# The tables of an S5 layer: spread rows read back by DMA, or products with states on partitions and a transpose on TensorE

## The chip, the cores and the metric

One Trainium2 chip, one of its cores. The metric is the device time of one launch in microseconds (us). The engines are called TensorE (PE in the profile, its weight loads PEld), VectorE (DVE), ScalarE (ACT), GpSimd (POOL) and SyncE (SP); each works through its own list of instructions in order and waits on semaphores for the others. SyncE only issues DMAs here; GpSimd computes and issues DMAs as well.

## The reference

One inference step of a decoder of two layers, for 256 prompt tokens and 8 samples of one token (264 columns in all), model width 2048, in float32. Layer 0 mixes with retention and HGRN2 heads, layer 1 with S5; after each mixer comes a SwiGLU FFN of width 5632.

The S5 layer has 128 groups of 16 channels with 64 complex states each:

```
dt = exp(log_dt);  a = exp(lam * dt);  b' = ((a - 1) / lam) * b      (complex, for each group and state)
h[t] = a * h[t-1] + b' u[t]                                          (u: 16 channels of the group)
y[t] = Re(c h[t]) + d * u[t]
```

followed by a GELU and a gated linear layer (GLU). The kernel doesn't scan token by token. It takes chunks of 8 tokens and makes two tables for each group out of a, b', c: `wb` takes the 8 x 16 inputs of a chunk to its 64 complex states and to the chunk's own outputs, `wc` takes the states to the outputs of the next 8 tokens.

## The kernel before

**The stream.** All large products run as one stream of units through `Step.stream` (lines 102 to 135). A unit is up to 8 blocks of 128x128 weights, 512 KB. SyncE loads it into one of 4 buffers `raw` (`load`, L82); ScalarE rounds it to the matmul format, `whi` (L88), and the rest `wlo = raw - whi` is made by VectorE, or by GpSimd for every `S.every`-th unit (`split`, L95). TensorE then does three matmuls a block on 264 columns (L126, L127, L129). `ahead` keeps splits up to 4 units and loads up to 8 units in front of the unit in work. Results are taken from PSUM by VectorE (gate L1544, up L1551 to L1554, w_dn L1559).

**Tasks beside the stream.** After each unit `Step.slot` calls every active generator once (`next`). A generator writes a few instructions into the engines' lists and yields. So the number of yields sets beside which unit a piece of work stands; a unit is all that lies between two calls.

**The first FFN** has 272 units: 64 of gate and up, 32 of w_dn, 64, 32, 48, and 32 short ones (6 blocks). Beside it runs `s5_tables` (L810), then the first part of `s5` (L1182), which loads finished tables back for the S5 stage. `s5_tables` makes, in this order:

- a, b' and their factors for all groups, states on partitions, 64 columns (two groups' states fill the 128 partitions); `S.every = 3` from here on;
- the rotations `rot`, 32 powers of a unit number (L938 to L965), wide products on VectorE;
- the powers of a, `pw`, and their products with the states' factor, `pdc`; these are transposed (L988) and written to DRAM (`pdd`); the coefficients b with the norm's gain, made on GpSimd (L1002), go to DRAM too (`btd`);
- `S.every = 0`, and the samples' part (a h0, L1014 to L1066);
- a loop over 16 groups of tables (`kt`), 8 S5 groups each, 9 calls a pass (5 in the first).

In a pass, GpSimd makes `bb` (b' with the gain) from the loaded coefficients `bc`; VectorE makes `T`, the table from states to tokens (L1151 to L1164), which goes to DRAM as `wc` (L1170). `through` (L1091) multiplies `bz` and `T` on TensorE (L1097) to the block within the chunk, `kp`, written to DRAM in 8 pieces (L1106). `spread` (L1084) lets SyncE load two tiles of 128x1024, `us` (a row of `pdd` for each token, the same on 16 partitions) and `vs` (a row of `btd` for each channel, repeated for 8 tokens); `tokens` (L1109) multiplies them on VectorE, complex, to the part of wb from tokens to states, which is written to DRAM as it stands (L1118), a piece of it to `bn` (L1122).

**After the stream,** `s5` makes the tokens' norm factors; while it waits, 10 matmuls on a tile of constants are put on TensorE (L1277). The S5 stage loads `wb` and `wc` through SyncE into whatever buffers are free.

Of the kernel before, what the change touches and what calls it, by code (L numbers as in the profile page):

```python
# [10 lines left out]
F32 = mybir.dt.float32  # L11
# [35 lines left out]
class Step:  # L47
    """The chip's state while the program is written out: pools, the stream of weights, the tasks beside it."""
# [183 lines left out]
def layer0(S, I, O):  # L232
# [206 lines left out]
    # the heads' products of earlier with later tokens, [(earlier), chunk, later]; never written above the diagonal  # L439
# [6 lines left out]
    def hg_head(h, H):  # L446
# [9 lines left out]
        def decay(l):  # L456
            """Takes the pairs of blocks to blocks of 2^l: the left keys to the block's end, the right queries to its start."""
# [154 lines left out]
    # the first four blocks together: they wait for the norm anyway  # L612
# [3 lines left out]
    # head start  # L616
# [192 lines left out]

def s5_tables(S, I):  # L810
    """The S5 layer's tables, beside the first FFN: chunks of 8 tokens, for each of the 128 groups
    from tokens to states and within the chunk (wb), and from states to tokens (wc)."""
# [52 lines left out]
    # sine and cosine - 1 of a quarter of the angle, doubled twice  # L865
# [59 lines left out]
    # the multiplier of a chunk and the unit rotations of its phase  # L925
# [4 lines left out]
    yield  # L930
# [3 lines left out]
    rot = S.rot  # L934
    G.memset(rot[:, 0, :, 0:1], 1.0)
    G.memset(rot[:, 1, :, 0:1], 0.0)
    cc, k = col("cc"), col("a0")
    n = 1  # L938
    while n < 32:
        # back to length 1, or its errors would grow with the chunks  # L940
        ts(cc, cm, 1.0, None, op0=OP.add)
        V.tensor_mul(p, cc, cc)
        V.tensor_mul(k, s, s)
        V.tensor_add(p, p, k)
        ts(p, p, -0.5, 1.5, op0=OP.mult, op1=OP.add)
        V.tensor_mul(s, s, p)
        V.tensor_mul(cc, cc, p)
        ts(cm, cc, -1.0, None, op0=OP.add)
        yield
        if n == 1:  # L950
            V.tensor_copy(rot[:, 0, :, 1:2], one(cc))
            V.tensor_copy(rot[:, 1, :, 1:2], one(s))
        else:
            w = min(n, 8)
            slow = n > 4
            for off in range(0, n, w):
                t = [new(f"rt{i}", [128, 64, 8])[:, :, :w] for i in range(2)]
                bc = lambda v: one(v).to_broadcast([128, 64, w])
                for _ in cmul(V, [rot[:, i, :, n + off:n + off + w] for i in range(2)],
                              [rot[:, i, :, off:off + w] for i in range(2)], (bc(cc), bc(s)), t):  # L960
                    if slow:
                        yield
        n *= 2
        if n < 32:
            double(s, cm)  # L965
            yield
    # powers of a
# [5 lines left out]
    # what wb takes from the states and what it takes from the channels, turned and spread by DMA:  # L973
    # the powers, falling with the token, times the states' factor
    pd, pdc = (new(n, [128, 2, KT, 8, 4]) for n in ("pd", "pdc"))
    for j in range(8):
        A.activation(pd[:, :, :, j], pw[:, :, :, 7 - j].rearrange("p i (k q) -> p i k q", q=4), AF.Copy)
        if j % 4 == 3:
            yield
    t = [new(f"rt{i}", [128, 64, 8]).rearrange("p a b -> p (a b)").rearrange("p (k j q) -> p k j q", j=8, q=4)  # L980
         for i in range(2)]
    cb = [v.rearrange("p (k o q) -> p k o q", o=1, q=4).to_broadcast([128, KT, 8, 4]) for v in (cr, ci)]
    yield from cmul(V, [pdc[:, i] for i in range(2)], [pd[:, i] for i in range(2)], cb, t)
    pdt = pd.rearrange("p i k j q -> p (i k j q)").rearrange("p (b r i s) -> p b r i s", b=4, r=2, i=2)
    for b in range(4):
        p = S.pt()
        for i in range(2):
            PE.transpose(p[:, 128 * i:128 * i + 128], pdc[:, i, 4 * b:4 * b + 4].rearrange("p k j q -> p (k j q)"), S.ident)  # L988
        A.activation(pdt[:, b], p[:, :256].rearrange("p (i r s) -> p r i s", i=2, r=2), AF.Copy)
        yield  # L990
    pdd = S.dr.tile([KT, 8, 1024], F32, name="pdd", bufs=1)
    G.dma_start(bass.AP(tensor=pdd.tensor, offset=pdd.offset, ap=[[256, 128], [32768, 4], [1, 256]]),
                pdt.rearrange("p b r i s -> p b (r i s)"))
    gt = new("gt", [128, KT])
    G.dma_start(gt, I["s5g"])
    btd = S.dr.tile([KT, 16, 1024], F32, name="btd", bufs=1)
    for b in range(4):
        bt = new(f"rt{b % 2}", [128, 64, 8]).rearrange("p a b -> p (a b)").rearrange("p (k x) -> p k x", k=4)
        G.dma_start(bt, I["s5b"][:, 4 * b:4 * b + 4])
        yield  # L1000
        yield
        G.tensor_mul(bt, bt, gt[:, 4 * b:4 * b + 4].rearrange("p (k o) -> p k o", o=1).to_broadcast([128, 4, 128]))  # L1002
        G.dma_start(bass.AP(tensor=btd.tensor, offset=btd.offset + 65536 * b, ap=[[128, 128], [16384, 4], [1, 128]]), bt)
# [24 lines left out]
    for h in range(2):  # L1028
# [34 lines left out]
    ym = new("rt0", [128, 64, 8])[:, :32].rearrange("p (k r) s -> p k r s", r=2)  # L1063
# [3 lines left out]
    inner.close()  # L1067
    inner = ExitStack()
    mp[0] = inner.enter_context(S.tc.tile_pool(name="s5k", bufs=1))
    # the tables, four pairs of groups at a time  # L1070
    bz = [new(f"bz{i}", [128, 2, 4, 2, 16]) for i in range(2)]
    kp = [new(f"kp{i}", [128, 240]) for i in range(2)]
    k0 = new("k0", [128, KT, 16])
    for i in range(2):
        G.memset(bz[i], 0.0)
        G.memset(kp[i], 0.0)
    S.wb, S.wc, S.bn = [], [], []

    def coefs(kt):
        bc = new("bc", [128, 5, 4, 16], 2)  # L1080
        G.dma_start(bc, I["s5t"][kt])
        return bc
# [8 lines left out]
    def through(kt, Tt):  # L1091
        """What of the tables takes the tensor engine: the chunk's blocks."""
        Bz, Kp = bz[kt % 2], kp[kt % 2]
        p = S.pt()
        for q in range(4):
            for i in range(2):
                PE.matmul(p[32 * q:32 * q + 32, :128], Bz[:, i, q].rearrange("p r c -> p (r c)"),  # L1097
                          Tt[:, i, q, :8].rearrange("p e c -> p (e c)"), start=i == 0, stop=i == 1,
                          tile_position=(0, 32 * q))
        A.activation(Kp[:, 112:], p[:, :128], AF.Copy)  # L1100
        stt(Kp[:, 112:128], mask16, dcol[:, kt:kt + 1], Kp[:, 112:128], op0=OP.mult, op1=OP.add)  # L1101
        A.activation(k0[:, kt], Kp[:, 112:128], AF.Copy)
        yield
# [708 lines left out]
```

## Time and profile before

| | us |
|---|---|
| median of three runs | 2497.26 (2496.51 to 2500.04) |
| span of the profiled execution | 2498.5 |
| TensorE busy | 2393.0 (96%) |
| VectorE busy | 1637.5 (66%) |
| ScalarE busy | 1090.1 (44%) |
| GpSimd busy | 480.7 (19%) |

The profile is of one execution; its span lies within the three times, and no time of that execution is given but the span. Busy time of TensorE is that of overlapping matmuls with modelled ends: a stretch without a gap reads as fully busy at either clock, so the granted clock is read beside it. DMA share is the mean busy share of the 16 DMA engines.

### The profile page before, as it was taken

Reading aid. Unit: us, or ns where it says so; the run is one execution under the profiler, and the core shown is the slowest. Engines: PE = TensorE matmul, PEld = TensorE weight load, DVE = VectorE, ACT = ScalarE, POOL = GpSimd, SP = SyncE. Lnnn points to the kernel's source line nnn. Section 1 sums busy time; section 2 is a strip of 40 time slices with the busy share of each in tenths; the row PEclk is TensorE's granted clock in tenths of the full one; section 3 lists DMA queues with packets and bytes.
Section 4 is the critical chain, followed back from the end, with each engine's and each line's share of the span. In section 5 each row is a group of like instructions: output and inputs, shape, how many; then the busy total and the mean of one; then the engine's idle time right before and its main releaser. Section 6 shows DMA issues by size and latency. Waiting matters only on the chain.

```text
span 2498.5 us, 48937 instructions
## 1 busy us (share of the span) xinstructions
PE 2393.0 (96%) x19958; PEld 2336.7 (94%) x19958; DVE 1637.5 (66%) x2553; ACT 1090.1 (44%) x1574; POOL 480.7 (19%) x629
## 2 busy tenths in 40 slices
PE   8999999999899998899988988999999999999997
PEld 8999999999899998889888957999999999999997
DVE  6777777768985677676666677555555555545555
ACT  6464555454343333333333445444344344433444
POOL 3112122222234144344433242000000000000000
PEclk9999999999999999999999998999999999999999
DMA  7766666764456788788887897555556555565554
GB/s 239 240 213 229 227 236 199 240 216 164 150 184 222 209 235 241 229 245 249 246 231 224 262 286 193 190 185 194 189 179 184 184 180 183 178 186 184 179 165 141
DMA packets 168352, 519.03 MB, mean 208 GB/s; under 512 B 23152, under 2 KB 42096, under 8 KB 167616
## 3 DMA queue, kind: packets, MB, share of 16 engines
q1 hardware_dynamic: 141552, 443.39, 56.3%
q0 software_dynamic: 26576, 72.52, 9.4%
q8 instruction: 157, 2.57, 0.4%
q14 instruction: 67, 0.55, 0.1%
HBM read 470.28 MB, written 45.48 MB: 206 GB/s over the span
## 4 chain that ended last, share of the span: by engine, by line
PE 69%; DVE 11%; DMA 10%; ACT 4%; issue 4%; POOL 1%; SPq 0%; DVEq 0%; ACTq 0%; POOLq 0%
PE acc L126 21%; PE acc L127 21%; PE acc L129 21%; DMA raw<-w_gu 6%; DVE wlo L95 4%; ACT whi L88 3%; DMA raw<-w_dn 1%; PE pa L487 1%; DMA wcp<-wc 1%; DMA wb<-kp 1%; DMA raw<-w_in 0%; DVE st L426 0%; POOL wb L1106 0%; DMA whi<-wb 0%; PE ps L318 0%
## 5 line engine op out<-in xcount | busy, mean ns | idle before, releaser
L95 DVE TENSOR_TENSOR wlo<-raw,whi 128x1024 fp32r<-128x1024 f32 (+1 forms) x722 | 877.3, 1219 | 518.9 <-ACT whi L88 517.6
L126 PE MATMUL acc<-xh,whi 128*128 128x264 f32 x3776 | 1093.4, 290 | 42.7 <-DVE up L1551 15.2
L129 PE MATMUL acc<-xh,wlo 128*128 128x264 f32 x3776 | 1079.3, 286 | 10.3 <-DVE wlo L95 6.0
L127 PE MATMUL acc<-xl,whi 128*128 128x264 f32 x3776 | 1076.0, 285 | 0.0
L88 ACT ACTIVATE whi<-raw 128x1024 fp32r<-128x1024 f32 (+1 forms) x767 | 784.3, 1035 | 503.1 <-PE acc L127 254.1
L126 PEld LDWEIGHTS acc<-xh,whi 128*128 128x128 f32 x3776 | 718.5, 190 | 50.9 <-issue 33.3
L129 PEld LDWEIGHTS acc<-xh,wlo 128*128 128x128 f32 x3776 | 715.4, 189 | 14.6 <-DVE wlo L95 8.7
L127 PEld LDWEIGHTS acc<-xl,whi 128*128 128x128 f32 x3776 | 719.4, 191 | 0.4
L126 PE MATMUL acc<-a2h,whi 128*128 128x264 f32 x2080 | 597.1, 287 | 7.4 <-DVE kp L1101 6.2
L129 PE MATMUL acc<-a2h,wlo 128*128 128x264 f32 x2080 | 592.7, 285 | 4.3 <-POOL wlo L95 2.8
L127 PE MATMUL acc<-a2l,whi 128*128 128x264 f32 x2080 | 592.7, 285 | 0.0
L126 PEld LDWEIGHTS acc<-a2h,whi 128*128 128x128 f32 x2080 | 395.1, 190 | 10.3 <-issue 8.4
L129 PEld LDWEIGHTS acc<-a2h,wlo 128*128 128x128 f32 x2080 | 393.4, 189 | 5.0 <-POOL wlo L95 3.0
L127 PEld LDWEIGHTS acc<-a2l,whi 128*128 128x128 f32 x2080 | 395.2, 190 | 0.0
L95 POOL TENSOR_TENSOR wlo<-raw,whi 128x1024 fp32r<-128x1024 f32 x45 | 112.1, 2494 | 290.2 <-ACT whi L88 270.8
L1553 ACT ACTIVATE a2h<-up 128x264 fp32r<-128x264 f32 x88 | 37.3, 424 | 264.8 <-DVE up L1552 264.8
L170 ACT ACTIVATE sg<-pre 128x264 f32<-128x264 f32 x88 | 37.4, 425 | 246.3 <-DVE pre L1544 246.3
L1721 POOL TENSOR_TENSOR xh<-xh,R 128x528 f32<-128x528 f32 x2 | 2.9, 1464 | 725.7 <-DVE R L181 725.7
L1106 POOL DMA_DIRECT2D wb<-kp x128 | 76.7, 607 | 162.3 <-DVE kp L1101 162.3
L1559 DVE TENSOR_TENSOR x<-x,acc 128x264 f32<-128x264 f32 x96 | 41.0, 427 | 49.6 <-PE acc L129 48.6
L1554 DVE TENSOR_TENSOR a2l<-up,a2h 128x264 fp32r<-128x264 f32 x88 | 40.9, 465 | 43.3 <-ACT a2h L1553 43.3
L1551 DVE TENSOR_TENSOR up<-acc,R 128x264 f32<-128x264 f32 x88 | 37.7, 428 | 32.5 <-PE acc L129 32.5
(479 smaller groups left out, 1885.6 us busy)
## 6 DMA issues: line engine op xcount, KB each, us to landing
raw<-w_gu SPq DMA_DIRECT2D x352, 512.0 KB
raw<-w_dn SPq DMA_DIRECT2D x128, 512.0 KB
raw<-w_in SPq DMA_DIRECT2D x127, 512.0 KB
raw<-w_glu SPq DMA_DIRECT2D x64, 512.0 KB
raw<-w_dn SPq DMA_DIRECT2D x64, 384.0 KB
raw<-w_out SPq DMA_DIRECT2D x32, 512.0 KB
st<-sret POOLq DMA_DIRECT2D x16, 512.0 KB, 8.1
o_sret<-st POOLq DMA_DIRECT2D x16, 512.0 KB, 6.5
```

The lines of the kernel that those rows point to most:

```text
L88: self.nc.scalar.activation(u.hi, u.raw, AF.Copy)
L95: e.tensor_sub(u.lo, u.raw, u.hi.bitcast(F32))
L126: mm(k.acc, u.hi[:, j], h, start=k.done == 0, stop=False)
L127: mm(k.acc, u.hi[:, j], l, start=False, stop=False)
L129: mm(k.acc, u.lo[:, j], h, start=False, stop=k.done == k.total)
L170: self.nc.scalar.activation(out, in_, func, **kw)
L487: PE.matmul(pa[:, at + 64 * j:at + 64 * j + 64], k[:, sl], q[:, sl].rearrange("p (b t s) -> p b t s", t=2, s=1 << l)[:, :, 1, :], start=Tr ...
L1106: G.dma_start(d[16 * j:16 * j + 16, :, 128:].rearrange("c g x -> g c x"), Kp[:, 16 * (7 - j):16 * (7 - j) + 128])
L1551: V.tensor_mul(t, acc, R)
L1553: A.activation(S.a2h[:, k], t, AF.Copy)
L1554: V.tensor_sub(S.a2l[:, k], t, S.a2h[:, k].bitcast(F32))
L1559: V.tensor_add(S.x[:, nt], S.x[:, nt], acc)
```

## The change

1. The loop over `kt` stands before the rotations and the samples' part, right behind the powers. The rotations become a generator, `turns`, one step of which is called at three places of a pass; the samples' part follows the loop, with buffers of its own.
2. `pdc`, its transposes, `pdd`, `btd` and `spread` are gone, and two inputs with them (s5b, s5g). In their place ScalarE copies the falling powers to `fall`.
3. The part of wb from tokens to states, `W`, is made by VectorE from `bb` and `fall` with states on partitions, six operations on 512 columns. `through` turns it: 8 transposes of 128x128 on TensorE into two PSUM tiles, and two copies by ScalarE into `wbt`, which is written to DRAM as before.
4. A pass has 11 calls. `through` of a pass is spread over six calls of the next (`tick`); the pieces of `kp`, `wbt` and `bn` are written in the last of them, `wc` one call later.
5. `S.every` is 4 from the loop on and is not set again, so GpSimd makes the wlo of every fourth unit to the kernel's end.
6. The matmuls before the norm are 13 on up to 512 columns of a tile left over from the stream (`S.wide`), no longer 10 on 128.

```
+    fall = keep("fall", [128, 2, 64, 8])
     for j in range(8):
+        A.activation(fall[:, :, :, j:j + 1], pw[:, :, :, 7 - j:8 - j], AF.Copy)
...
+    def through(kt, Tt, W):
+        yield
...
+        A.activation(Kp[:, 112:], p[:, :128], AF.Copy)
+        stt(Kp[:, 112:128], mask16, dcol[:, kt:kt + 1], Kp[:, 112:128], op0=OP.mult, op1=OP.add)
+        A.activation(k0[:, kt], Kp[:, 112:128], AF.Copy)
+        yield
+        yield
...
+        w = new("wbt", [128, 1024])
+        wv = w.rearrange("p (q r i s) -> p i q r s", q=4, r=2, i=2)
         for i in range(2):
+            p = S.pt()
+            for q in range(4):
+                PE.transpose(p[:, 128 * q:128 * q + 128], W[:, i, q].rearrange("p j c -> p (j c)"), S.ident)
+            A.activation(wv[:, i], p.rearrange("p (q r s) -> p q r s", q=4, r=2), AF.Copy)
+            yield
+        for j in range(8):
+            G.dma_start(d[16 * j:16 * j + 16, :, 128:].rearrange("c g x -> g c x"),
+                        Kp[:, 16 * (7 - j):16 * (7 - j) + 128])
+        G.dma_start(d[:, :, :128], w.rearrange("p (g x) -> p g x", g=8))
...
+    S.every = 4
+    pend = []
+    def tick(turn=False):
+        for g in list(pend):
+            if next(g, "end") == "end":
+                pend.remove(g)
+        if turn:
+            next(turns, None)
+    for kt in range(KT):
...
+        W = new("W", [128, 2, 4, 8, 16])
+        B, P = [exp4(bb[:, i], 8) for i in range(2)], [pow4(fall[:, i, q4], 8) for i in range(2)]
+        t = scratch(8)
+        V.tensor_mul(t[0], B[0], P[0])
+        V.tensor_mul(t[1], B[1], P[1])
+        yield
+        V.tensor_sub(W[:, 0], t[0], t[1])
+        tick(True)
+        yield
...
+        pend.append(through(kt, Tt, W))
...
-    S.every = 0
...
-    def spread(kt):
-        u, v = (new(n, [128, 1024]) for n in ("us", "vs"))
-        nc.sync.dma_start(u, bass.AP(tensor=pdd.tensor, offset=pdd.offset + 8192 * kt, ap=[[1024, 8], [0, 16], [1, 1024]]))
-        nc.sync.dma_start(v, bass.AP(tensor=btd.tensor, offset=btd.offset + 16384 * kt, ap=[[0, 8], [1024, 16], [1, 1024]]))
-        return [x.rearrange("p (g i s) -> p g i s", g=8, i=2) for x in (u, v)]
...
-    for i in range(10):
-        PE.matmul(idle[:, 128 * (i % 4):128 * (i % 4) + 128], S.onesD, S.onesD, start=True, stop=True)
+    for i, n in enumerate((4, 4, 4, 4, 3, 3, 3, 3, 1, 1, 1, 1, 1)):
+        PE.matmul(idle[:, :128 * n], S.wide[:, i % 2], S.wide[:, 2:2 + n].rearrange("p k c -> p (k c)"), start=True, stop=True)
...
     ffn(S, I, 0, after_ffn0)
     S.stream()
     S.drain()
+    S.wide = S.units[-1].lo
```

## Rows read from the trace of the kernel before

**Rows 1.** Windows by stage: stretch and length, engines' busy us, TensorE clock, DMA share, GB/s.

```profile
569.00:1455.00 886.00, 824.66 (x6778) 804.89 (x6777) 622.92 (x930) 336.47 (x494) 305.92 (x438) 0.97 0.74 223
640.00:725.00 85.00, 76.60 (x611) 74.39 (x611) 75.81 (x135) 32.04 (x45) 21.37 (x9) 1.00 0.48 161
725.00:866.00 141.00, 136.38 (x1216) 134.19 (x1215) 82.88 (x95) 56.41 (x72) 44.00 (x50) 0.99 0.68 212
866.00:1375.00 509.00, 463.57 (x3774) 451.72 (x3773) 351.73 (x476) 182.86 (x280) 207.81 (x343) 0.95 0.82 237
...
1455.00:1540.00 85.00, 64.64 (x738) 42.19 (x737) 71.04 (x91) 40.45 (x76) 42.07 (x39) 0.90 0.95 241
1560.00:2480.00 920.00, 920.00 (x7602) 918.55 (x7601) 512.85 (x621) 394.26 (x498) 5.18 (x4) 1.00 0.57 181
1600.00:1650.00 50.00, 50.00 (x416) 50.00 (x415) 28.03 (x35) 23.64 (x35) 0.00 (x0) 1.00 0.54 181
```

**Rows 2.** Windows of 4 us within one pass of the loop.

```profile
1004.00:1008.00 4.00, 4.00 (x35) 4.00 (x34) 0.00 (x0) 0.00 (x0) 0.00 (x0) 1.00 1.02 275
1008.00:1012.00 4.00, 0.68 (x6) 0.47 (x4) 0.09 (x1) 1.06 (x1) 0.00 (x0) 0.90 0.56 209
1012.00:1016.00 4.00, 2.38 (x11) 2.41 (x12) 2.12 (x4) 2.19 (x5) 1.34 (x3) 0.50 0.56 187
```

**Rows 3.** The chain of waits in that pass: start, us, what.

```profile
993.46 1.22 SPq L1088
...
994.77 15.94 DMA raw<-w_gu
```

**Rows 4.** DMA issues of the loop, 866 to 1375: count, size, us to landing.

```profile
us<-pdd SPq DMA_DIRECT2D x16, 512.0 KB
vs<-btd SPq DMA_DIRECT2D x16, 512.0 KB
wc<-T POOLq DMA_DIRECT2D x16, 512.0 KB, 10.9
wb<-kp POOLq DMA_DIRECT2D x128, 64.0 KB, 3.8
wb<-wbt POOLq DMA_DIRECT2D x16, 512.0 KB, 5.3
```

**Rows 5.** TensorE's timeline: a chunk block, and a pair of transposes: start, us, what.

```profile
1067.45 0.67 PE L1097 MATMUL pt<-T,bz 128*32 128x128 f32 x16
...
1398.52 0.28 PE L129 MATMUL acc<-a2h,wlo 128*128 128x264 f32 x1
1398.86 0.48 PE L1658 MATMUL pt<-ident,xl 128*128 128x128 f32 x2
1399.10 0.37 PE L126 MATMUL acc<-a2h,whi 128*128 128x264 f32 x1
```

**Rows 6.** TensorE's timeline at a pair of the transposes of pdc.

```profile
738.87 0.29 PE L129 MATMUL acc<-xh,wlo 128*128 128x264 f32 x1
738.99 0.38 PE L988 MATMUL pt<-ident,pdc 128*128 128x128 f32 x2
739.13 0.37 PE L126 MATMUL acc<-xh,whi 128*128 128x264 f32 x1
739.33 0.28 PE L127 MATMUL acc<-xl,whi 128*128 128x264 f32 x1
```

**Rows 7.** VectorE by line in the loop: count, busy us, mean ns, idle before.

```profile
L95 DVE TENSOR_TENSOR wlo<-raw,whi 128x1024 fp32r<-128x1024 f32 x144 | 177.9, 1236 | 137.7 <-ACT whi L88 136.8
...
L799 DVE TENSOR_TENSOR t<-us,vs 128x512 f32<-128x512 f32 x16 | 10.9, 684 | 0.0
```

**Rows 8.** Timelines of VectorE and GpSimd around 659.

```profile
658.95 0.69 DVE L799 TENSOR_TENSOR rt<-rot,cc 128x512 f32<-128x512 f32 x1
659.56 2.86 DVE L800 TENSOR_TENSOR rt<-rot,a 128x512 f32<-128x512 f32 x1
...
658.97 2.90 POOL L95 TENSOR_TENSOR wlo<-raw,whi 128x1024 fp32r<-128x1024 f32 x1 [12.68 <-ACT whi L88]
```

More of the change, by code (lines that the diff above doesn't have):

```diff
@@ L933, in s5_tables @@
     yield
[L934 to L966, printed above, removed]
     for o, n in ((2, 1), (3, 2), (5, 4)):
@@ L982, in s5_tables @@
[L982 to L985, printed above, removed]
-        p = S.pt()
[L987 to L999, printed above, removed]
+    rs, rcm, rar, rai = (keep(n, [128, 64]) for n in ("rs", "rcm", "rar", "rai"))
@@ new lines, in s5_tables, with rotations @@
+    for o, i in ((rs, s), (rcm, cm), (rar, ar), (rai, ai)):
+        A.activation(o, i, AF.Copy)
+    yield
+    inner.close()
+    inner = ExitStack()
+    mp[0] = inner.enter_context(S.tc.tile_pool(name="s5k", bufs=1))
+    def rotations():
+        rot, s, cm = S.rot, rs, rcm
+        cc, k, p = col("cc"), col("rk"), col("rp")
+        G.memset(rot[:, 0, :, 0:1], 1.0)
+        G.memset(rot[:, 1, :, 0:1], 0.0)
+        n = 1
+        while n < 32:
+            ts(cc, cm, 1.0, None, op0=OP.add)
+            V.tensor_mul(p, cc, cc)
+            V.tensor_mul(k, s, s)
+            yield
+            V.tensor_add(p, p, k)
+            ts(p, p, -0.5, 1.5, op0=OP.mult, op1=OP.add)
+            yield
+            V.tensor_mul(s, s, p)
+            V.tensor_mul(cc, cc, p)
+            ts(cm, cc, -1.0, None, op0=OP.add)
+            yield
+            if n == 1:
+                V.tensor_copy(rot[:, 0, :, 1:2], one(cc))
+                V.tensor_copy(rot[:, 1, :, 1:2], one(s))
+            else:
+                w = min(n, 8)
+                for off in range(0, n, w):
+                    t = [new(f"rt{i}", [128, 64, 8])[:, :, :w] for i in range(2)]
+                    bc = lambda v: one(v).to_broadcast([128, 64, w])
+                    yield from cmul(V, [rot[:, i, :, n + off:n + off + w] for i in range(2)],
+                                    [rot[:, i, :, off:off + w] for i in range(2)], (bc(cc), bc(s)), t)
+            n *= 2
+            if n < 32:
+                stt(p, cm, 1.0, s, op0=OP.add, op1=OP.mult)
+                stt(cm, s, -2.0, s, op0=OP.mult, op1=OP.mult)
+                ts(s, p, 2.0, None, op0=OP.mult)
+                yield
@@ new lines, in s5_tables, with coefs @@
+    turns = rotations()
+    bz = [new(f"bz{i}", [128, 2, 4, 2, 16]) for i in range(2)]
+    kp = [new(f"kp{i}", [128, 240]) for i in range(2)]
+    k0 = new("k0", [128, KT, 16])
+    for i in range(2):
+        G.memset(bz[i], 0.0)
+        G.memset(kp[i], 0.0)
+    S.wb, S.wc, S.bn = [], [], []
+    exp4 = lambda v, n: v.rearrange("p q (o c) -> p q o c", o=1).to_broadcast([128, 4, n, 16])
+    pow4 = lambda v, n: v.rearrange("p q (e o) -> p q e o", o=1).to_broadcast([128, 4, n, 16])
+    def coefs(kt):
+        bc = new("bc", [128, 5, 4, 16], 2)
+        G.dma_start(bc, I["s5t"][kt])
+        return bc
@@ new lines, in through @@
+    def through(kt, Tt, W):
+        yield
+        Bz, Kp = bz[kt % 2], kp[kt % 2]
+        p = S.pt()
+        for q in range(4):
+            for i in range(2):
+                PE.matmul(p[32 * q:32 * q + 32, :128], Bz[:, i, q].rearrange("p r c -> p (r c)"),
+                          Tt[:, i, q, :8].rearrange("p e c -> p (e c)"), start=i == 0, stop=i == 1,
+                          tile_position=(0, 32 * q))
+        A.activation(Kp[:, 112:], p[:, :128], AF.Copy)
+        stt(Kp[:, 112:128], mask16, dcol[:, kt:kt + 1], Kp[:, 112:128], op0=OP.mult, op1=OP.add)
+        A.activation(k0[:, kt], Kp[:, 112:128], AF.Copy)
@@ new lines, in s5_tables @@
+    S.every = 4
[7 more added lines that the diff above has]
+    for kt in range(KT):
+        q4 = slice(4 * kt, 4 * kt + 4)
+        if kt == 0:
+            bc = coefs(0)
+            for _ in range(3):
+                yield
+        else:
+            bc = nxt
+        nxt = coefs(kt + 1) if kt < KT - 1 else None
+        bb = new("bb", [128, 2, 4, 16], 2)
+        tm = [new(f"tb{i}", [128, 4, 16]) for i in range(2)]
+        c2 = [one(v[:, q4]).to_broadcast([128, 4, 16]) for v in (cr, ci)]
+        for _ in cmul(G, [bb[:, i] for i in range(2)], [bc[:, i] for i in range(2)], c2, tm):
+            pass
+        G.tensor_mul(bb, bb, bc[:, 4:].to_broadcast([128, 2, 4, 16]))
+        A.activation(bc[:, 3], bc[:, 3], AF.Copy, scale=-1.0)
+        C, P = [exp4(bc[:, 2 + i], 9) for i in range(2)], [pow4(pw[:, i, q4], 9) for i in range(2)]
+        Tt = new("T", [128, 2, 4, 9, 16], 2)
+        scratch = lambda n: [new(f"t{i}", [128, 4, 9, 16])[:, :, :n] for i in range(2)]
+        t = scratch(9)
+        V.tensor_mul(t[0], C[0], P[0])
+        tick()
+        yield
+        V.tensor_mul(t[1], C[1], P[1])
+        tick()
+        yield
+        V.tensor_add(Tt[:, 0], t[0], t[1])
+        tick()
+        yield
+        t = scratch(9)
+        V.tensor_mul(t[0], C[1], P[0])
+        tick()
+        yield
+        V.tensor_mul(t[1], C[0], P[1])
+        tick()
+        yield
+        V.tensor_sub(Tt[:, 1], t[0], t[1])
+        tick()
+        yield
+        Bz = bz[kt % 2]
+        for h in range(2):
+            A.activation(Bz[64 * h:64 * h + 64, :, :, h], bb[64 * h:64 * h + 64], AF.Copy)
+        d = S.dr.tile([128, 2, 4, 128], F32, name=f"wc{kt}", bufs=1)
+        G.dma_start(d, Tt[:, :, :, 1:9].rearrange("p r q e c -> p r q (e c)"))
+        S.wc.append(d)
+        tick(True)
+        yield
+        W = new("W", [128, 2, 4, 8, 16])
[3 more added lines that the diff above has]
+        V.tensor_mul(t[1], B[1], P[1])
+        yield
+        V.tensor_sub(W[:, 0], t[0], t[1])
+        tick(True)
+        yield
+        t = scratch(8)
+        V.tensor_mul(t[0], B[0], P[1])
+        V.tensor_mul(t[1], B[1], P[0])
+        yield
+        V.tensor_add(W[:, 1], t[0], t[1])
+        tick(True)
+        yield
+        pend.append(through(kt, Tt, W))
@@ L1004, in s5_tables @@
+    while pend:
+        tick(True)
+        yield
+    S.k0 = S.dr.tile([128, KT, 16], F32, name="k0d", bufs=1)
+    G.dma_start(S.k0, k0)
+    for _ in turns:
+        yield
+    inner.close()
+    inner = ExitStack()
+    mp[0] = inner.enter_context(S.tc.tile_pool(name="s5h", bufs=1))
     cts = {}
@@ L1036, in s5_tables @@
             yield
-        t = [new(f"rt{i}", [128, 64, 8])[:64].rearrange("p a b -> p (a b)").rearrange("p (a b) -> p a b", a=8)
-             for i in range(2)]
+        t = [new(f"rt{i}", [64, 8, 64]) for i in range(2)]
         ah = new("ah", [64, 8, 2, 64])
@@ L1066, in s5_tables @@
     V.tensor_add(S.y0, ym[:, :, 0], ym[:, :, 1])
[L1067 to L1082, printed above, removed]
@@ L1084, in spread @@
-    def spread(kt):
-        u, v = (new(n, [128, 1024]) for n in ("us", "vs"))
-        nc.sync.dma_start(u, bass.AP(tensor=pdd.tensor, offset=pdd.offset + 8192 * kt, ap=[[1024, 8], [0, 16], [1, 1024]]))
-        nc.sync.dma_start(v, bass.AP(tensor=btd.tensor, offset=btd.offset + 16384 * kt, ap=[[0, 8], [1024, 16], [1, 1024]]))
-        return [x.rearrange("p (g i s) -> p g i s", g=8, i=2) for x in (u, v)]
[L1091 to L1103, printed above, removed]
-        d = S.dr.tile([128, 8, 256], F32, name=f"wb{kt}", bufs=1)
-        for j in range(8):
-            G.dma_start(d[16 * j:16 * j + 16, :, 128:].rearrange("c g x -> g c x"),
-                        Kp[:, 16 * (7 - j):16 * (7 - j) + 128])
-        S.wb.append(d)
@@ L1173, in s5_tables @@
-    for _ in range(3):
-        yield
-    yield from pending
-    S.k0 = S.dr.tile([128, KT, 16], F32, name="k0d", bufs=1)
-    G.dma_start(S.k0, k0)
     inner.close()
```

86 lines of the change are left out of this document (13 added, 73 removed).

## The prediction

> **What bounds the kernel now.** I read the windows by stage first. In a stretch that has only the stream of weights, TensorE is busy all the time at full clock: 416 matmuls in 50 us, 0.1202 us each, so a unit of 24 costs 2.885 us, while the DMA engines are busy 0.54 of the time [rows 1]. The whole second half is of that kind. The first FFN is not. It has 272 units, 240 of 24 matmuls and 32 of 18, so 6,336 matmuls or 761.6 us at that pace; it runs from 569 to 1455, 886 us [rows 1]. The small matmuls put into the stream are worth some 29 us, an estimate: 16 chunk blocks at 0.8 (0.67 and the change over), 16 transposed rows at 0.55 [rows 5], and some 7 for the samples' products and the norm. So about 95 us are lost in this one stage, and the change works in this stage.
>
> Where they are lost: in 866 to 1375, the loop over the 16 groups of tables, TensorE is busy 463.57 of 509 us and its mean granted clock is 0.95; that is 45 us idle and some 25 us of work not done at half clock, 70 us. In 640 to 725, where the rotations are made, 8.4 us are idle while VectorE is busy 75.81 of 85 us (0.89). In 725 to 866, 4.6 us idle and about 1.4 by the clock [rows 1]. Together 85 us that could be had.
>
> The cause in the loop is seen within one pass. The DMA engines are full from 1004 to 1008, TensorE has 0.68 of 4 us from 1008 to 1012 and 2.38 us from 1012 to 1016 at clock 0.50 [rows 2]. The chain of waits says what is late: SyncE issues the spread load vs (L1088, right behind that of us), then the next load of weights, and this takes 15.94 us to land [rows 3]. What else moves in the loop, each pass: us and vs at 512 KB each on SyncE's own queue, ahead of the weights, and 512 KB each of wb<-wbt, of wc<-T and (as 8 pieces) of wb<-kp on GpSimd's queue [rows 4]. So TensorE waits for weights behind a burst of some 2 MB, runs dry, and begins again at half clock.
>
> **The change part by part.** *Removed: the spread.* 32 loads of 512 KB leave SyncE's queue. The loop now takes 11 calls a pass where it took 9 (5 in the first), and one call comes with each unit: 11 units of 512 KB and about 1.7 MB of table traffic give 7.3 MB per pass of some 34 us, 215 GB/s, against 237 GB/s in the loop today [rows 1]. The burst (wb<-kp, wb<-wbt and wc<-T fall within two calls) is 1.5 MB, none of it on the weights' queue. At the 275 GB/s seen with full DMA engines [rows 2] that is 5.5 us, against the 11.5 us of four loaded units. I take it that the 70 us come back but for a residue of 8 (a tenth); bounds 0 and 35 (half the stall stays, as the burst is 1.5 of 2.5 MB).
>
> *Moved: the rotations.* They go from a stretch of their own into the loop, one small step per call at three calls of eleven; the 8.4 us of 640 to 725 and most of the 6 of 725 to 866 (rows bt multiplied on GpSimd, products pdc) come back: 14. With the 70 this is 84, and the eight transposes of pdc save 1: 85.
>
> *Added on TensorE: 8 transposes of 128x128 a pass, 128 in all, in groups of four.* Two bounds from pairs. In the transposed rows a pair sits between matmuls that start at 1398.52 and 1399.10: 0.58 instead of 0.12, and the next gap 0.21, so 0.55 extra [rows 5]. For pdc, matmuls start at 738.87, 739.13 and 739.33 with a pair among them: 0.46 where two steps are 0.24, so 0.22 extra, 0.11 for each [rows 6]. A group of four is thus 0.44 to 0.77 (the 0.33 between the two pairs paid once a group), 32 groups 14 to 25 us. The 0.55 paid for each pair would be 35. I take 20. These are on the path, as TensorE is the bound.
>
> The Trainium skill says of a PE-mode transpose (TensorE: Matmul & The Clock Gate, section PE-mode transpose) that one took about 275 ns within a kernel. By that, an estimate, 128 would be 35 us and the sum 15 us worse; the trace shows starts some 0.11 us apart, so duration is not cost here, and I stay with the rows.
>
> *Added on VectorE.* The six operations that make wb's token part stay six, on as many columns (128x512, 0.684 us [rows 7]), only with states on partitions. Their results pass PSUM and two ScalarE copies a pass; ScalarE is busy 182.86 of 509 us, so these are hidden; without that cover, at VectorE's 0.684 us for as many columns, 1.4 us a pass or 22 in all.
>
> *Moved to GpSimd: every fourth wlo,* from the loop on and to the end of the kernel (S.every = 4 is never taken back; today 0 from the samples' part on). This is the term that speaks against the change. At 658.97 GpSimd begins a wlo of 2.90 us; VectorE's product that begins at 659.56 takes 2.86 us, where the like one before took 0.69 [rows 8]. So one wlo moved takes 1.236 us off VectorE [rows 7] and puts 2.17 on it: 0.23 us a unit more, not less. VectorE today has 351.73 us for 147 units, 2.39 each [rows 1], of which the tables are 1.0 (six operations a pass at 0.684 [rows 7], six on 576 columns, so some 0.8 each, and a small one: 9.2 us over 9.2 units, an estimate). After: 2.39 - 0.31 + 0.54 - 1.0 + 0.84 (9.2 over 11 calls) + 0.2 (rotations, an estimate: 18 operations like that of 0.69 [rows 8] and some sixty narrower ones, 25 us over some 125 units) = 2.66 us, about 2.76 in gate and up units, which do more with their results than those of w_dn (0.1 more, an estimate). In 640 to 725 VectorE came no further than 0.89 busy, so 2.76 asks for 3.10 us a unit; TensorE asks for 2.885 + (0.8 + 1.25)/11 = 3.07. The two are level, and level engines wait on each other. I take 0.14 us for each of 113 gate and up units in the loop, 16 us. Bounds: 0, if the four units of lead absorb it; 45, if a unit takes 3.47 as today's do (509 over 147).
>
> The Trainium skill has the stall as a rule (SBUF — State Buffer, section SBUF: two separate sides): a GpSimd instruction and a VectorE one with two SBUF inputs exclude each other for the whole instruction. The trace agrees: 2.86 against 0.69 us. Were it shared bandwidth instead, the 16 would be near 0 and the sum 16 us better.
>
> *Past the first FFN.* In GLU and the second FFN VectorE is busy 512.85 of 920 us and TensorE all of it [rows 1]; 84 wlo moved, each with 0.9 us more for VectorE, stay far below its limit: 0, bounds 0 and +5. The tables end at call 239 of 272 where they ended at 236, the preloads for S5 at 272 instead of 269. The S5 stage has its DMA engines 0.95 busy [rows 1], so a load that started later would cost there; but SyncE only follows its own list and waits for no call: 0, bounds 0 and +7 (three short units). The warm-up products before S5 change form within a wait for the norm: 0, at most 2 either way.
>
> **Sum:** 85 - 20 - 16 - 8 = 41 us gained. The profiled execution has a span of 2498.5, 1.2 above the median of 2497.26 and within the three times; taken off the median, **2456 us**. The likeliest case's own range, 20 to either side with a little more above (14 to 25 for the transposes, 5 to 30 for VectorE, 0 to 20 for the burst, not all at one end): 2436 to 2482.
>
> **Rivals.** *VectorE is not crowded and the burst harmless:* 85 less only the 14 to 25 of the transposes, so 2426 to 2437. For it: calls hold one or two table operations each, evenly spread. Against it: the 0.89 of 640 to 725.
>
> *The stall stays in another form:* 45 for VectorE leaves 85 - 20 - 45 - 8 = 12; 35 for the burst with 25 for the transposes leaves 9; some of both leaves nothing: 2482 to 2502. For it: the writes of 512 B pieces stay, and now fall together.
>
> *GpSimd becomes late (slower than before).* Its instructions go in order, and it is busy 207.81 us in the loop, 13 a pass, with issues and the multiplications of bb [rows 1]; 2.75 wlo add about 8 (2.90 each [rows 8]). If a wlo stood behind a whole pass of that work, 16 us would go by, while a unit has four units, 11.5 us, of lead. If that struck in each pass, 4.4 us idle and as much again at half clock would be 8.8 x 16 = 140 us, against the 65 won (85 less 20): 2572 at worst. It decides from 4 us a pass on, idle and slow clock together. Behind the late wlo stand wb's and wc's issues, which nothing in this stage waits for, and the buffer raw, so the next load. Against it: the issues and bb lie some five calls apart, so the lead is won back between, and of the wlo at most one in four lies right behind the issues.
>
> **How the numbers follow.** Likeliest 0.56; uncrowded 0.16; stall in another form 0.18; GpSimd late, or late tables that hit S5, 0.10. A difference under 0.2% (5 us) can't be told from no change. Faster by more: 0.56 + 0.16 + two thirds of 0.18, less a little for the unknown, 0.82; same 0.09; slower 0.09. The range 2428 to 2497 leaves out the slower case and a few hundredths at either end.
>
> **What the changed profile would show.** Right: in the loop (now some 665 to 1230) no load of weights of 15 us, clock near 1.00, TensorE over 0.97 busy, 128 transposes some 0.11 apart, 3.1 to 3.3 us a unit; VectorE at 0.85 or more with operations of 2.9 us wherever GpSimd has a wlo; the first FFN some 845 us. Wrong, if TensorE waits there for wlo of GpSimd (GpSimd late), if loads still take over 12 us (burst), if TensorE idles after results on VectorE (crowding larger), or if the S5 stage grows from 85 us.

## The result, and the profile after

The changed kernel takes 2434.51 us (median of 4 runs, 2429.6 to 2437.19) where the kernel before took 2496.89 beside it (2495.62 to 2500.04): ratio 0.9747, 95% interval 0.9733 to 0.976, 63 us less. The forecast was 2456 with a range of 2428 to 2497; the time lies in the range, 21 us under the forecast and just under the likeliest case's own range.

Windows of the kernel after: the loop with the tables, the part of the samples, the S5 stage, and GLU with the second FFN. Columns as in [rows 1]: stretch and length, busy us of TensorE, its weight loads, VectorE, ScalarE and GpSimd (x instructions), TensorE clock, DMA share, GB/s.

```profile
660.00:1230.00 570.00, 567.02 (x4843) 560.73 (x4843) 452.13 (x588) 246.62 (x366) 335.09 (x403) 1.00 0.69 223
1230.00:1320.00 90.00, 84.91 (x790) 83.00 (x789) 47.42 (x62) 38.13 (x53) 27.61 (x29) 0.96 0.62 186
1389.00:1474.00 85.00, 64.95 (x731) 42.74 (x731) 72.20 (x90) 40.17 (x76) 44.17 (x40) 0.89 0.96 245
1494.00:2414.00 920.00, 920.00 (x7602) 918.55 (x7602) 420.39 (x542) 394.47 (x499) 192.94 (x84) 1.00 0.57 181
```

The loop, 463.57 of 509 us at clock 0.95 before [rows 1], is now 567.02 of 570 at 1.00. The next window has a new loss: 5.1 us idle, and 0.04 of 90 us by the clock. TensorE does in the two later stages what it did. The last addition to the residual stream in the first FFN starts at 1389.1 us, where it started at 1455.16: 66 us, so the whole gain lies in that one stage.

DMA issues of the loop after, 660 to 1230. The loads of weights land in 4.3 us; none takes the 15.94 us of [rows 3]. The longest of those loads takes 7.6. What is left of the burst of [rows 4] is there and stalls nothing.

```profile
raw<-w_gu SPq DMA_DIRECT2D x124, 512.0 KB, 4.3
...
wc<-T POOLq DMA_DIRECT2D x16, 512.0 KB, 6.3
wb<-kp POOLq DMA_DIRECT2D x128, 64.0 KB, 4.9
wb<-wbt POOLq DMA_DIRECT2D x16, 512.0 KB, 6.5
```

The four transposes of one group on TensorE's timeline. The matmul ahead starts at 1015.74 and the one behind at 1016.21: 0.47 where one step is 0.12, and the next step is 0.21 instead of 0.12, so 0.44 extra for the group. That is the lower of the prediction's two bounds.

```profile
1015.74 0.28 PE L129 MATMUL acc<-xh,wlo 128*128 128x264 f32 x1
1015.86 0.60 PE L1030 MATMUL pt<-ident,W 128*128 128x128 f32 x4
1016.21 0.37 PE L126 MATMUL acc<-xh,whi 128*128 128x264 f32 x1
1016.42 0.28 PE L127 MATMUL acc<-xl,whi 128*128 128x264 f32 x1
```

VectorE, and below it GpSimd, in one pass of the loop after.

```profile
1003.47 0.69 DVE L1112 TENSOR_TENSOR t<-bb,fall 128x512 f32<-128x512 f32 x1
1004.40 3.11 DVE L95 TENSOR_TENSOR wlo<-raw,whi 128x1024 fp32r<-128x1024 f32 x1 [0.24 <-ACT whi L88]
1007.43 0.78 DVE L1114 TENSOR_TENSOR W<-t,t 128x512 f32<-128x512 f32 x1
```

```profile
1003.32 3.11 POOL L95 TENSOR_TENSOR wlo<-raw,whi 128x1024 fp32r<-128x1024 f32 x1
1006.38 0.57 POOL L1004 DMA_DIRECT2D bc<-s5t  x1
```

VectorE's wlo, 1.236 us alone [rows 7], takes 3.11 while GpSimd has one of its own and ends about 1.1 us after it. So the stall of [rows 8] is there; TensorE hardly feels it, with 2.98 us idle in the whole loop, as VectorE is busy only 452.13 of 570 us, 0.79.

GpSimd's timeline where TensorE now loses time: its wlo of 1244.09 stands behind a row of small transfers that wait for each other.

```profile
1236.78 0.55 POOL L1133 DMA_DIRECT2D ct<-s5c  x1 [3.39 <-DMA k0d<-k]
1237.32 2.05 POOL L1145 DMA_DIRECT2D ad<-at  x4
1239.36 0.56 POOL L1150 DMA_DIRECT2D mask<-mask  x1
1240.90 0.60 POOL L1154 DMA_DIRECT2D a<-ad  x1 [0.98 <-DMA ad<-at]
1242.89 0.57 POOL L1154 DMA_DIRECT2D a<-ad  x1 [1.39 <-DMA ad<-at]
1243.46 0.62 POOL L1157 DMA_DIRECT2D h<-s5h  x1
1244.09 2.36 POOL L95 TENSOR_TENSOR wlo<-raw,whi 128x1024 fp32r<-128x1024 f32 x1
```

### The profile page after: what moved, and what is told of

The parts are those of the page before. It is cut to its first block, busy times and chain, and to the rows that moved or that the text cites. A ratio compares the mean times of both kernels' runs of the same rounds, so it can differ in the third digit from the quotient of the medians.

```text
span 2432.4 us, 49004 instructions
## 1 busy us (share of the span) xinstructions
PE 2379.1 (98%) x20071; PEld 2330.7 (96%) x20071; DVE 1538.1 (63%) x2416; ACT 1107.0 (46%) x1606; POOL 779.0 (32%) x746
## 4 chain that ended last, share of the span: by engine, by line
PE 81%; DVE 9%; ACT 4%; issue 3%; DMA 2%; POOL 1%; SPq 0%; DVEq 0%; ACTq 0%; POOLq 0%
PE acc L126 25%; PE acc L127 25%; PE acc L129 25%; DVE wlo L95 3%; ACT whi L88 2%; DMA wcp<-wc 1%; PE pa L487 1%; DMA wb<-kp 0%; DMA raw<-w_in 0%; DVE st L426 0%; POOL wlo L95 0%; PE pt L1030 0%; PE pt L1323 0%; PE pt L1015 0%; PE ps L318 0%
## 5 line engine op out<-in xcount | busy, mean ns | idle before, releaser
L95 DVE TENSOR_TENSOR wlo<-raw,whi 128x1024 fp32r<-128x1024 f32 (+1 forms) x591 | 733.4, 1243 | 375.0 <-ACT whi L88 374.9
L95 POOL TENSOR_TENSOR wlo<-raw,whi 128x1024 fp32r<-128x1024 f32 (+1 forms) x176 | 423.8, 2408 | 1242.0 <-ACT whi L88 1217.7
L1555 DVE TENSOR_TENSOR pre<-acc,R 128x264 f32<-128x264 f32 x88 | 37.8, 429 | 122.7 <-PE acc L129 122.5
```

The costliest lines, as they stand in the source:

```text
L95: e.tensor_sub(u.lo, u.raw, u.hi.bitcast(F32))
L1555: V.tensor_mul(t, acc, R)
```

## The experiments

The ratios are to the kernel before, run beside each kernel on the same chip. Two questions: what in the spread held the weights back, and which of the prediction's deductions were real.

**1. Before, without the spread.** us and vs are loaded in the first pass alone; 30 loads are left out, and the tables are not the right ones.

```diff
-        u, v = (new(n, [128, 1024]) for n in ("us", "vs"))
-        nc.sync.dma_start(u, ...)
-        nc.sync.dma_start(v, ...)
+        if kt == 0:
+            rows[:] = [new(n, [128, 1024]) for n in ("us", "vs")]
...
+        u, v = rows
```

> The kernel before, but the spread rows us and vs are loaded in the first pass alone and every later pass multiplies these same rows: 30 of the 32 loads of 512 KB are left out, and the tables they should have made are not made. Nothing else moves. Theory (the loop's 70 us are lost because these loads stand in front of the weights' loads on SyncE's queue, within a burst that fills the DMA engines): 55 to 70 us faster, 2427 to 2442, granted clock of the loop near 1.00. Rival (the loop is held by VectorE's work or by the other writes): within 15 us of the kernel before.

2426.01 us, 0.9709 (0.9693 to 0.9724): 73 us, somewhat more than the 70 read off as idle time and slow clock. The window of its loop:

```profile
866.00:1313.00 447.00, 447.00 (x3851) 441.62 (x3851) 362.08 (x488) 193.14 (x288) 215.52 (x360) 1.00 0.77 242
```

TensorE has no gap left and the full clock, and nothing else was touched, so these loads are the whole of the loop's loss.

**2. Before, the same loads on GpSimd's queue.**

```diff
-        nc.sync.dma_start(u, ...)
-        nc.sync.dma_start(v, ...)
+        G.dma_start(u, ...)
+        G.dma_start(v, ...)
```

> The kernel before with the same 32 loads of us and vs issued by GpSimd's queue instead of SyncE's: the same bytes, but no longer ahead of the weights on their queue. If the order on the queue is what costs: 30 to 60 us faster, 2437 to 2467. If the bytes alone cost (full DMA engines): within 12 us of the kernel before, 2485 to 2509. GpSimd gets some 0.6 us more for each load, 19 us in all, hidden as nothing in that loop waits for its wlo.

2437.26 us, 0.9753 (0.9738 to 0.9769), as fast as the whole change. DMA issues of this run's loop, 866 to 1313, and its window:

```profile
vs<-btd POOLq DMA_DIRECT2D x16, 512.0 KB, 12.7
...
us<-pdd POOLq DMA_DIRECT2D x15, 512.0 KB, 11.0
```

```profile
866.00:1313.00 447.00, 443.85 (x3792) 435.61 (x3792) 352.17 (x478) 187.22 (x280) 223.01 (x375) 1.00 0.91 271
```

The same bytes move, at 271 GB/s and not 237 [rows 1], and TensorE has work for all but 3.2 us. So the bytes are not the main cost (some 11 us are left over experiment 1, by the ratios); that the weights stand behind these loads is. And these loads are slow: 11 and 12.7 us for 512 KB.

**3. After, with two loads of 512 KB a pass put back on SyncE's queue**, of distinct rows, copied to DRAM and not used.

```diff
+        for n in ("us", "vs"):
+            d = S.dr.tile([128, 8, 128], F32, name=f"{n}{kt}", bufs=1)
+            nc.sync.dma_start(d, I["w_dn"][1, kt, :, 0:8])
```

> The changed kernel with two copies of 512 KB a pass added on SyncE's queue, DRAM to DRAM with rows of 4 KB, whose data nobody uses; they stand where the loads us and vs stood in a pass. If the burst on the weights' queue is the cause, it comes back in part, as a pass is now 11 units long and not 9: 15 to 50 us slower than the changed kernel, 2450 to 2485, with loads of weights over 10 us. If spreading the work over more calls is what helped: 2434 to 2442.

2436.1 us, 0.9752 (0.9735 to 0.9769). The stall did not come back, and the theory that 1 MB more ahead of the weights is enough fell, for copies to DRAM; experiment 4 asks it of loads into the tiles.

**4. Before, with us and vs loaded from distinct rows**: same place, size and tiles, other data (the tables are not right).

```diff
-        nc.sync.dma_start(u, bass.AP(... ap=[[1024, 8], [0, 16], [1, 1024]]))
-        nc.sync.dma_start(v, bass.AP(... ap=[[0, 8], [1024, 16], [1, 1024]]))
+        for i, x in enumerate((u, v)):
+            nc.sync.dma_start(x.rearrange("p (k c) -> p k c", k=8), I["w_dn"][1, kt, :, 8 * i:8 * i + 8])
```

> The kernel before, with us and vs loaded at the same place on SyncE's queue, of the same 512 KB and into the same buffers, but each partition reads 4 KB of its own from w_dn and not one of 8 or 16 rows that all read (the tables are not right). Theory A (the spread loads are slow because 128 partitions read the same few rows, and hold back the weights behind them): the loads land in some 6 us as the distinct ones of the added-loads run did (6.5), the stall goes, 2426 to 2445 us. Theory B (1 MB more in front on the weights' queue is enough, whatever it reads): the stall stays, 2485 to 2500 us. In between: both have a share, read off from where it lies.

2426.38 us, 0.9713 (0.97 to 0.9727): as if the loads were not there. Windows, then DMA issues, of this run's loop:

```profile
866.00:1313.00 447.00, 447.00 (x3851) 441.62 (x3850) 361.08 (x487) 194.45 (x289) 212.82 (x358) 1.00 0.83 277
```

```profile
raw<-w_gu SPq DMA_DIRECT2D x108, 512.0 KB, 5.2
...
us<-w_dn SPq DMA_DIRECT2D x16, 512.0 KB, 6.5
vs<-w_dn SPq DMA_DIRECT2D x16, 512.0 KB, 7.4
```

More bytes per microsecond than in the kernel before, on the same queue in the same order, and no stall. So it is how the spread loads were formed. Three things changed at once here: the rows are distinct, the access pattern of the source has 128 as its outermost size and not 8, and the source is w_dn and not pdd and btd.

**5 to 7. The spread's form, put elsewhere.** Copies of few rows read many times over (same patterns, outermost size 8), to DRAM and not used: in the kernel after between the table's products (5); there again but right behind the store wb<-wbt, where the kernel before had them (6); and in the kernel before at the old place, for the 30 later loads (7, whose tables are not right).

```diff
+        src = I["w_dn"][1, kt]
+        for n, ap in (("us", [[5632, 8], [0, 16], [1, 1024]]), ("vs", [[0, 8], [5632, 16], [1, 1024]])):
+            d = S.dr.tile([128, 1024], F32, name=f"{n}{kt}", bufs=1)
+            nc.sync.dma_start(d, bass.AP(tensor=src.tensor, offset=src.offset, ap=ap))
```

> The kernel after, with two unused 512 KB copies a pass on SyncE's queue whose sources are 8 and 16 rows of 4 KB read 16 and 8 times, as us and vs read them (the run with distinct rows gave 2436.1). Theory A (re-read rows make the load slow): the copies take over 10 us to land, weights behind them come late, and the time is 2450 to 2490 us. Theory B (the reads make no difference): 2433 to 2442 us, as with distinct rows.

> The kernel after with the two copies of re-read rows again (2447.7 in the run before, 12 above the distinct ones), but issued right behind the store wb<-wbt, where the kernel before has us and vs. If it is the meeting with the writes of wb that makes the spread as dear as it was before (72 us), 2465 to 2500; if the place makes no difference, 2443 to 2452, and what is left lies in where the loads write or in what waits for them.

> The kernel before with the 30 later spread loads, of the same re-read rows at the same place on SyncE's queue, writing to DRAM and not to the tiles us and vs (the tables are made from the first pass's rows). If the re-reading at this place is the cost whatever it writes to, and no wait for the tiles has a part, 2480 to 2500; if writing to SBUF or SyncE's wait for the tiles is needed for the stall, 2426 to 2450, as in the kernel after with such copies added (2447.7).

2447.67 us, 0.9799 (0.9785 to 0.9812); 2442.18, 0.9763 (0.9744 to 0.9782); 2444.64, 0.9771 (0.9753 to 0.9788). The time of 5 lies between its two ranges, that of 6 just under its second, that of 7 in its second. The form costs 13 us over the kernel after in 5 and 15 over experiment 1 in 7, by the ratios; the 4 us in 6 lie within the intervals. So for copies to DRAM the meeting with wb's stores adds nothing (6 is not dearer than 5, and that idea fell). But it costs far less than the 73 us of the loads into the tiles.

**What the trace of before says of the form.** Windows of the kernel before, a microsecond each, and its queues from 1009 to 1012 (packets, MB, share of the 16 engines; q1 is SyncE's queue, q0 GpSimd's):

```profile
1009.00:1010.00 1.00, 0.00 (x0) 0.00 (x0) 0.00 (x0) 0.00 (x0) 0.00 (x0) 1.00 0.51 205
1010.00:1011.00 1.00, 0.00 (x0) 0.00 (x0) 0.00 (x0) 0.18 (x1) 0.00 (x0) 1.00 0.51 205
1011.00:1012.00 1.00, 0.00 (x0) 0.00 (x0) 0.09 (x1) 0.87 (x1) 0.00 (x0) 0.61 0.51 205
```

```profile
q1 hardware_dynamic: 171, 0.61, 51.0%
q0 software_dynamic: 1, 0.00, 0.0%
```

TensorE has nothing to do, SyncE's queue alone is at work, and the share stands at one half: 205 GB/s at 0.51 is 402 GB/s for a full set, against 277 at 0.83, or 334, in experiment 4. In these microseconds the busy engines are not slow; half of them have nothing left. The trace's single packets say the same: eight are in flight at nearly every moment, of 4 KB and some 160 ns each. Of the loop's 45.4 us of idle TensorE, 32.3 lie in microseconds with a share of 0.44 to 0.56; in experiment 4 none does, and in 5 to 7 between 0.2 and 3.6 us do. The reading, argued and not tested: a spread load keeps 8 of the 16 engines, its outermost size, and the parts of the next loads that fall to those 8 wait behind it while the other 8 run dry.

The Trainium skill has this as a rule (DMA: Bandwidth & Descriptors, section Why a DMA increments its semaphore by 16 and not by 1): a copy is split over as many engines, 16 at most, as divide the outermost size of both its patterns. The share of 0.51 agrees.

That is when TensorE starves; it is not the whole cause. Ahead of the half-empty stretch all 16 engines are busy, and slow. Windows some 5 to 11 us behind an issue of us, of before (issued at 992.81), of experiment 4 (1002.00) and of experiment 2 (1008.58):

```profile
1000.00:1004.00 4.00, 4.00 (x44) 3.66 (x44) 3.40 (x5) 1.38 (x2) 1.31 (x4) 1.00 1.05 223
```

```profile
1008.00:1009.00 1.00, 1.00 (x10) 1.00 (x10) 0.51 (x3) 0.93 (x3) 1.00 (x3) 1.00 1.06 420
1009.00:1010.00 1.00, 1.00 (x11) 1.00 (x10) 1.00 (x2) 0.99 (x2) 0.92 (x3) 1.00 1.01 414
```

```profile
1014.00:1018.00 4.00, 4.00 (x45) 3.66 (x44) 3.35 (x4) 2.18 (x4) 3.24 (x5) 1.00 1.06 234
```

At the same share the engines carry 223 GB/s in before and 414 to 420 in experiment 4. Means over the 15 later passes, 4 to 14 us behind the issue of us, say the same:

| | DMA share | GB/s |
|---|---|---|
| before | 1.01 | 246 |
| 2, on GpSimd's queue | 1.02 | 268 |
| 4, distinct rows | 0.99 | 372 |
| 7, to DRAM | 0.91 | 326 |

A pass thus loses twice. By what is not moved (an estimate): 126 GB/s less than in experiment 4 over 10 us, 1.3 MB, and then in before about half a set, 195 GB/s at a share of 0.50, over the 4 us from 16 to 20, 0.8 MB. The slow stretch is the larger part. On GpSimd's queue the engines are as slow and TensorE loses 3.2 us in all, so slow engines alone don't starve it: the weights must stand behind these loads as well.

What stays open: no run changed the outermost size alone with the rows re-read as they were, or the rows alone, so which of the two makes the engines slow is not shown. The 13 to 15 us into DRAM and the 73 into the tiles go with the rate, 326 GB/s at 0.91 and 246 at 1.01; why a tile as the destination makes it so low is not known.

**8. After, without the 128 transposes.** ScalarE copies W unturned, so wb's token part is not turned.

```diff
-            p = S.pt()
-            for q in range(4):
-                PE.transpose(p[:, 128 * q:128 * q + 128], W[:, i, q]..., S.ident)
-            A.activation(wv[:, i], p.rearrange(...), AF.Copy)
+            A.activation(wv[:, i], W[:, i]..., AF.Copy)
```

> The changed kernel without the 128 transposes on TensorE: ScalarE copies W as it lies into wbt, so wb's token part is left unturned. Prices the transposes. By the prediction's term 14 to 25 us faster than the changed kernel, 2410 to 2421; by what is left over when the gain of 66 us in the first FFN is taken from the 86 that could be had, less the idle time still seen there, 5 to 9 us, 2425 to 2430.

2425.25 us, 0.9705 (0.9688 to 0.9723): the transposes cost some 10 us (0.0042 of 2497; 9.3 by the spans, 2432.4 and 2423.1), 0.3 for a group of four. TensorE stands idle 5.70 of the loop's 570 us in this run and 2.98 in the kernel after, so some 3 us more of its time were freed and lost again to waits.

**9, 10. After, wlo back on VectorE**: from the loop on (9), or from the part of the samples on alone (10).

```diff
-    S.every = 4
+    S.every = 0
```

In 10 `S.every = 4` stays, and this is added where the part of the samples begins:

```diff
+    S.every = 0
     cts = {}
```

> The kernel after with every wlo from the loop on made on VectorE, none on GpSimd (S.every is 0 where it was 4). VectorE was 0.79 busy in the loop (2.57 us a unit, of which the stalls by GpSimd's wlo are a part). Theory (moving wlo to GpSimd brought nothing, since each puts 2.17 us on VectorE and takes 1.24 off): VectorE's busy time in the loop falls by some 30 to 50 us, TensorE has as little idle time as now, and the 8 us lost at the samples' part (GpSimd's wlo behind a late load) come back: 2422 to 2432. Rival (VectorE was near its limit and GpSimd's share relieves it): TensorE waits for wlo of VectorE in the loop, 2438 to 2460.

> The kernel after with every fourth wlo on GpSimd in the loop only, and none from the samples' part on (S.every = 0 there, as before the change). If the loss at 1232 to 1247 comes of GpSimd's wlo behind its wait for a load, TensorE is busy there all the time at full clock and the time falls by 5 to 9 us, to 2425 to 2430; if that loss has another cause, 2433 to 2437. Against the run with all of them on VectorE: the same if the loop does not mind GpSimd's wlo; slower by some us if it does.

2422.64 us, 0.9699 (0.9686 to 0.9712), and 2431.13, 0.9734 (0.9721 to 0.9747). Windows of experiment 9:

```profile
660.00:1230.00 570.00, 570.00 (x4878) 564.60 (x4878) 441.48 (x635) 250.88 (x371) 211.97 (x361) 1.00 0.72 225
1230.00:1320.00 90.00, 88.01 (x826) 85.74 (x826) 56.13 (x77) 40.83 (x59) 20.25 (x38) 1.00 0.69 197
```

With 46 more wlo of its own VectorE is busy 10.65 us less. 46 at 1.22 us are 56 us, so one on GpSimd cost VectorE (56 + 10.65)/46 = 1.45 us on average, more than the 1.22 it took off. The loop loses nothing now. In 10 my expectation missed: the loss at 1240 to 1256 stayed, with VectorE in GpSimd's place. The window and VectorE's timeline there:

```profile
1230.00:1320.00 90.00, 84.47 (x789) 82.41 (x787) 49.87 (x69) 36.46 (x51) 16.05 (x29) 0.98 0.66 191
```

```profile
1247.20 0.43 DVE L1566 TENSOR_TENSOR a2l<-up,a2h 128x264 fp32r<-128x264 f32 x1 [0.49 <-ACT a2h L1565]
1254.85 0.68 DVE L799 TENSOR_TENSOR rt<-a,h 64x512 f32<-64x512 f32 x1 [7.21 <-DMA h<-s5h]
1255.46 0.68 DVE L800 TENSOR_TENSOR rt<-a,h 64x512 f32<-64x512 f32 x1
1256.06 1.21 DVE L95 TENSOR_TENSOR wlo<-raw,whi 128x1024 fp32r<-128x1024 f32 x1
```

This price holds for the loop. In GLU and the second FFN the same move did free VectorE: busy 512.85 of 920 us before [rows 1] and 420.39 after, with 80 wlo moved, 1.16 us for each and so nearly its whole time.

In 10 VectorE stands 7.21 us before the samples' product, until h lands behind the transfers shown above, and the next wlo stands behind it.

**11. Experiment 9 with that product two calls later.**

```diff
-        for _ in range(3):
+        for _ in range(5 if h == 0 else 3):
```

> The kernel after with all wlo from the loop on made on VectorE (2422.6 in the run before) and the samples' first product put two calls later, so that VectorE does not stand before it (5.92 us there, waiting for the load of h, with wlo queued behind). TensorE lost 1.3 us there to wlo of VectorE and 2 us in all in that stretch: 2419 to 2422.5 us. If the two calls push the S5 stage's first loads back, 2423 to 2428.

2420.46 us, 0.9679 (0.9663 to 0.9695): the fastest of these kernels. VectorE's wait there is 1.26 us, and the window of 1230 to 1320:

```profile
1230.00:1320.00 90.00, 89.58 (x844) 87.72 (x843) 58.41 (x80) 41.71 (x61) 19.05 (x35) 1.00 0.68 199
```

Against 9 the intervals overlap; the spans (2421.6 and 2418.6) and the windows agree on some 2 to 3 us.

**12. Before, no wlo on GpSimd while the small tables and the rotations are made.**

```diff
-    S.every = 3
+    S.every = 0
```

> The kernel before with no wlo on GpSimd while the small tables and the rotations are made (S.every = 0 from the start of the tables, where it was 3). If GpSimd's wlo, which stall VectorE's products (2.86 us for 0.69), are what makes VectorE late in the rotations, the 8 us idle there come back for the most part: 2486 to 2493 us. If the rotations themselves are too much for VectorE, taking 1.24 us for each wlo it gets back, the time stays or grows: 2497 to 2510.

2484.17 us, 0.9932 (0.9917 to 0.9946): 17 us, more than expected. Windows of this run:

```profile
640.00:725.00 85.00, 83.68 (x681) 82.44 (x680) 73.41 (x139) 35.24 (x50) 0.00 (x0) 1.00 0.54 177
725.00:866.00 141.00, 140.68 (x1277) 138.51 (x1276) 81.82 (x98) 56.73 (x70) 33.47 (x53) 1.00 0.74 224
```

VectorE takes over all wlo and is busy 73.41 us instead of 75.81 [rows 1]; TensorE has 83.68 of 85 where it had 76.60. The rotations never were too much for VectorE: GpSimd's wlo made them so.

## Why the prediction was right, and where its steps were off

**Where the loss lay, and that it comes back:** right. 85 us were read off; the two losses measure 73 (experiment 1) and 17 (12), 90 together.

**The cause in the loop:** wrong in part. "So TensorE waits for weights behind a burst of some 2 MB" names the right place, the weights behind the spread on SyncE's queue, and the wrong quantity. The same 2 MB cost TensorE 3.2 us in the loop if two loads go by another queue (2) and nothing if they are loads of another form (4). The rows that said it were in the prediction's own group: 0.56 from 1008 to 1016 with TensorE starved, and before it 275 GB/s at a share of 1.02 [rows 2], which I took for what full engines carry, where experiment 4 has 414 to 420. I read the full stretch of 1004 to 1008 as the burst and did not ask why the share then fell to half while weights were missing. As the change takes these loads away, the wrong quantity did not spoil the sign.

**Residue of the burst, 8:** it measured 0. The loop is full once wlo is off GpSimd (9), with all stores of [rows 4] still there. The term followed from the wrong quantity.

**Transposes, 20 of 14 to 25:** some 10. The extra at a group is 0.44, the lower bound, 14 us in all; of these some 3 come back as waits when the transposes are gone (8). The figure of the Trainium skill (TensorE: Matmul & The Clock Gate, section PE-mode transpose), 275 ns, agrees with the rows as a duration (271 to 273 ns each in the loop). The cost is less than half of that, 0.08 us each by the time and 0.11 by the starts; the prediction was right to stay with starts.

**VectorE and GpSimd, 16:** the size is nearly right (11 to 12, experiment 9), by luck, as the place is not. The price of 2.17 us, taken from one pair of operations, was 1.45 on average, so 1.45 - 1.22 = 0.2 us net and not 0.9, and crowding cost the loop 3 us and not 16: TensorE took 3.03 us a unit (570 over 188 loads), VectorE 2.40 (452.13 over 188) and not 2.66. The 0.89 of 640 to 725, which the prediction took for the most that VectorE can give, goes with GpSimd's wlo: without them TensorE is idle 1.3 us there and not 8.4 (12). The sign that VectorE would be at 0.85 or more did not come (0.79). The rest, some 7 us idle and by the clock, is the rival of the late GpSimd, which struck once, at the samples' part, and not in each pass; and behind it stands a wait for h that VectorE would have had itself (10).

**Past the first FFN, 0:** right, though not by the price given there: the wlo moved freed VectorE (420.39 us for 512.85) and did not load it. S5 has 64.95 busy of 85 us, as before; GLU and the second FFN have 920 of 920.

**The sum** with measured terms: 90 - 10 - 11 - 0 = 69, against 63 measured; the 6 left over are within the intervals of the terms. The forecast's 41 was short by 5 on what could be had, 10 on the transposes, 5 on VectorE and 8 on the burst, 28 in all, and long by those 6. The time fell where the first rival put it (2426 to 2437), and for its two reasons in the loop: the burst harmless, VectorE nearly uncrowded. That it fell there is in part luck: the 11 us of GpSimd's wlo and the 6 left over, which this rival has at 0, were nearly made up by 5 more that could be had and by transposes at 10 and not 20.

## What to carry to other kernels

When an engine starves, read the DMA share and the GB/s side by side, in steps of a microsecond. Here a full share with a low rate (223 GB/s at 1.05), and then a flat half with a full rate (205 at 0.51), told that the loads ahead were badly formed. Such a load's form is to be mended, or its queue changed, before its producer is rebuilt: two lines that move the spread to GpSimd's queue gained as much here as the whole change. And an elementwise operation given to GpSimd is to be priced stage by stage, by what VectorE is busy with and without it, not by the time that VectorE no longer spends on it.

## What the hardware showed unexpectedly

Thirty loads of 512 KB, two a pass, of few rows read many times over and with 8 as the outermost size, cost 73 us, and the same bytes on distinct rows nothing; while they were under way all 16 DMA engines were busy and carried 246 GB/s and not 372. GpSimd's wlo made VectorE busier, not freer, beside the tables in both kernels (441.48 us without 46 of them, 452.13 with them; 73.41 and 75.81 in the rotations), and freer in GLU and the second FFN (512.85 us without them, 420.39 with them).
